# Scores of two pairs of heads in one run of products, in a hybrid encoder trunk

## The chip, the cores and the metric

The kernel runs on one core of a Trainium2 chip. The metric is device time of one execution in microseconds (us). Engines are called PE (TensorE, matrix products), DVE (VectorE), ACT (ScalarE), POOL (GpSimd) and SP (SyncE, which issues the loads).

## The reference

Two layers over a sequence of 256 tokens with 1024 channels, in float32. Each layer projects its input once and gives the parts to three kinds of attention: 6 forgetting heads, 5 stick-breaking heads and 5 sparse heads with an indexer, all 64 wide. Their outputs are gated, merged and projected; a squared-ReLU MLP with a gated embedding follows.

```python
h = x @ w_in[i]
o_fox = fox_attention(fq, fk, fv, log_f)            # softmax(q k + c_q - c_k), causal
o_sb = stick_breaking_attention(sq, sk, sv)         # exp(log_sigmoid(z) + sum of log_sigmoid(-z'))
o_dsa = dsa_attention(dq, dk, dv, iq, ik, iw)       # softmax over the keys that an indexer picks
merged = (gates[:, :, 0] * (o_fox @ w_up_fox[i]) + gates[:, :, 1] * (o_sb @ w_up_sb[i])
          + gates[:, :, 2] * (o_dsa @ w_up_dsa[i]))
x = layer_norm(ALPHA * x + merged @ w_out[i])
ffn = square(relu(x @ w_ff_in[i])) @ w_ff_out[i]
x = layer_norm(ALPHA * x + ffn + sigmoid(x @ w_ple_gate[i]) * (p[i] @ w_ple[i]))
```

## The kernel before

Every product of two float32 matrices is made of three products of rounded halves (`mm3`, line 179): a high and a low part of each operand. ACT makes the high part (a cast, line 164), DVE the low part (a subtraction, line 165); `split` does both. Weights come in units through three rings of five buffers: `wr` (raw), `wh` (high), `wl` (low). So behind each unit on PE stand a load, a cast on ACT and a subtraction on DVE, and the cast waits until PE has given back the `wh` buffer of five units earlier.

PSUM has eight banks. Four are `pg`, the sums of the large projections; four are `ps`, for all small results: scores, transposes, values. `ps()` hands its four banks out in turn, so the fifth tile takes the bank of the first and has to wait until the last reader of that one is done.

The order of the work in a layer is built by generators. `gemm()` yields the units of the large projections in the order of `PRODUCTS`; a loop advances the jobs of the list `JOBS` by one step each for every 550 columns of projection (`PACE`). Jobs are `fox0`, `fox2`, `fox4` (forgetting heads 0 and 1, 2 and 3, 4 and 5), `sb0`, `sb2`, `sb4` (stick-breaking heads, two, two and one), `dsa0`, `dsa1`, `dsa3` (sparse heads 0; 1 and 2; 3 and 4), and others for the decay sums, the indexer and transposes. So small attention steps stand between the products of the weight stream on PE. Each engine then runs its own list in a fixed order.

The steps that matter here:

- The scores of a pair of heads. A head is 64 wide, so one product fills half of the rows of PE's array; `mm3s` (line 186) issues the products of two heads in turn, one on each half, into two `ps` banks. For forgetting and sparse heads this stands at the top of `softmax_heads`; for forgetting heads two further products (line 782) add the decay. For each query tile there are three products a head: first 128 keys wide, then 256. For stick-breaking heads it stands at the top of `sb_heads`.
- The softmax of a head (lines 787 to 794): DVE adds the mask and takes a minimum (787), ACT the exponential (790), DVE the reciprocal and the scaling (792, 794). Then PE transposes (line 199), ACT and DVE split, and `values` multiplies with v.
- Softplus and masks of a stick-breaking head (lines 879 to 886), on ACT, DVE and POOL.
- `values` for stick-breaking head 4 and sparse head 0 leaves its result in two `ps` banks; ACT copies it out (line 761) and DVE takes the rest of the low half (line 762).
- Rotations of the projections (lines 515 to 524) on DVE and POOL; line 573 is PE's product of the turned and split part.

The values of sparse head 0 and of stick-breaking head 4 are made just ahead of the scores of sparse heads 1 and 2; line 573 comes some 15 us after the scores of forgetting heads 2 and 3.

Of the kernel before, what the change touches and what calls it, by code (L numbers as in the profile page):

```python
# [10 lines left out]
F32 = mybir.dt.float32  # L11
# [5 lines left out]
P = 128  # L17
# [5 lines left out]
H_FOX, H_SB, H_DSA, H_IDX = 6, 5, 5, 8  # L23
# [29 lines left out]
def hybrid_trunk(ctx, tc, x, p, w_in, b_forget, w_up_fox, w_up_sb, w_up_dsa, w_out,  # L53
# [10 lines left out]
    def nm(s):  # L64
        uid[0] += 1
        return f"{s}_{uid[0]}"

    def ps():
        return psp.tile([P, 512], F32, tag="ps", name=nm("ps"), bufs=4)
# [24 lines left out]
    def small(w, dt=F32):  # L94
        return act.tile([P, w], dt, tag="small", name=nm("small"), bufs=24)
# [86 lines left out]
    def mm3s(outs, start, stop):  # L182

        for i in range(3):
            for o, a, b in outs:
                nc.tensor.matmul(o, a[i == 2], b[i == 1], start=start and i == 0, stop=stop and i == 2)  # L186
# [9 lines left out]
    def transpose_to(dst, src_list):  # L196

        for i, s in enumerate(src_list):
            tr = nc.tensor.transpose(dst[:, i * P:(i + 1) * P], s, ident)  # L199
            if pinned[0]:  # L200
                tc.keep_in_program_order(tr)
# [280 lines left out]
    mfox = cst.tile([P, 384], F32, name="mfox")  # L482
# [24 lines left out]
    for l in range(L):  # L507
# [158 lines left out]
        M = {}  # L666
# [101 lines left out]
        def t3k(dt=F32R):  # L768
            return act.tile([P, 2, 384], dt, tag="t3k", name=nm("t3k"), bufs=T3K)

        def softmax_heads(n, heads, mask, at_once=False):

            pr = t3k(F32)
            tiles = ((0, slice(0, P)), (1, slice(P, 3 * P)))
            ss = [ps() for _ in heads]
            for t, sl in tiles:
                nk = (t + 1) * P
                mm3s([(s[:, sl], [a[:, t * P:(t + 1) * P] for a in qT], [a[:, 0:nk] for a in kT])
                      for s, (qT, kT, _) in zip(ss, heads)], True, heads[0][2] is None)
                for s, (_, _, extra) in zip(ss, heads):  # L780
                    if extra is not None:
                        nc.tensor.matmul(s[:, sl], extra[0][:, t * P:(t + 1) * P], extra[1][:, 0:nk],
                                         start=False, stop=True)
            for i, s in enumerate(ss):
                mn = small(8)
                for t, sl in tiles:
                    nc.vector.tensor_tensor_reduce(pr[:, i, sl], s[:, sl], mask(t), 1.0, 3e38,
                                                   ALU.add, ALU.min, mn[:, t:t + 1])
                for t, sl in tiles:
                    nc.scalar.activation(pr[:, i, sl], pr[:, i, sl], AF.Exp, bias=mn[:, t:t + 1],  # L790
                                         scale=-1.0, accum_out=mn[:, 2 + t:3 + t])
                nc.vector.reciprocal(mn[:, 4:6], mn[:, 2:4])
                for t, sl in tiles:
                    nc.vector.tensor_scalar(pr[:, i, sl], pr[:, i, sl], mn[:, 4 + t:5 + t], None,
                                            op0=ALU.mult)
                yield
            pT = (t3k(), t3k())
            for i in range(len(heads)):
                q = ps()

                transpose_to(q, [pr[:, i, c * P:(c + 1) * P] for c in range(3)])
                split(q[:, 0:384], pT[0][:, i, :], pT[1][:, i, :])
                last[0] = pT[0].bitcast(F32)[:, i, 0:1]
                if not at_once or i == len(heads) - 1:
                    yield
            values(n, len(heads), pT)
            yield

        def fox_heads(h0):
            def part(i, h):  # L810
                r0 = (h % 2) * 64
                blk = i * 3 + h // 2
                return [a[r0:r0 + 64, (blk % 2) * T:(blk % 2 + 1) * T] for a in fT[blk // 2]]

            def sums(h):
                r = slice((h % 2) * 64, (h % 2) * 64 + 64)
                return sel[r, h // 2, :], cT[r, :]

            return softmax_heads(h0, [(part(0, h), part(1, h), sums(h)) for h in (h0, h0 + 1)],
                                 lambda t: mfox[:, 0:P] if t == 0 else mfox[:, P:3 * P])  # L820

        def dsa_heads(hs):
            def part(h):
                r0 = (h % 2) * 64
                if h < 4:
                    qT = [a[r0:r0 + 64, (h // 2) * T:(h // 2 + 1) * T] for a in dqT]
                else:
                    qT = [a[0:64, :] for a in dq4]
                return qT, [a[r0:r0 + 64, :] for a in dkT], None
            return softmax_heads(H_FOX + H_SB + hs[0], [part(h) for h in hs],  # L830
                                 lambda t: M[t][:, :(t + 1) * P], at_once=hs[-1] == H_DSA - 1)


        def sb_unit(kb):
# [19 lines left out]
        def strict(a, m):  # L854

            for i in range(m):
                v = a[:, i, :].rearrange("p (c t) -> p c t", t=P)[:, 0:3:2, :]
                nc.gpsimd.affine_select(out=v, in_=v, compare_op=ALU.is_gt, fill=0.0, base=0,
                                        pattern=[[0, 2], [1, P]], channel_multiplier=-1)

        def sb_heads(hs):
            m = len(hs)
            u, sp, sph, spl = t3k(F32), t3k(F32), t3k(), t3k()
            zs, qk = [ps() for _ in hs], []
            for h in hs:
                r0 = (h % 2) * 64
# [3 lines left out]
                else:  # L870
# [2 lines left out]
                  for z, (qT, kT) in zip(zs, qk)], True, True)  # L873
            mm3s([(z[:, T:T + P], [a[:, P:T] for a in kT], [a[:, P:T] for a in qT])
                  for z, (qT, kT) in zip(zs, qk)], True, True)
            for i, z in enumerate(zs):
                z = z[:, 0:384]
                e = u[:, i, :]
                nc.scalar.activation(e, z, AF.Abs)
                nc.scalar.activation(e, e, AF.Exp, scale=-1.0)  # L880
                nc.scalar.activation(e, e, AF.Ln, bias=1.0)
                nc.vector.scalar_tensor_tensor(sp[:, i, :], z, 0.0, e, op0=ALU.max, op1=ALU.add)
                nc.vector.scalar_tensor_tensor(e, z, 0.0, e, op0=ALU.min, op1=ALU.subtract)
                strict(sp[:, i:i + 1, :], 1)
                nc.scalar.copy(sph[:, i, :], sp[:, i, :])
                nc.vector.tensor_sub(spl[:, i, :], sp[:, i, :], sph[:, i, :].bitcast(F32))
                yield
# [28 lines left out]
        m = {}  # L916
# [111 lines left out]
        for h in (0, 2, 4):  # L1028
            jobs[f"fox{h}"] = (("fox", "fv"), lambda h=h: fox_heads(h))
        for hs in ((0, 1), (2, 3), (4,)):  # L1030
            jobs[f"sb{hs[0]}"] = (("sb", "sv"), lambda hs=hs: sb_heads(hs))
# [13 lines left out]
        while more or todo or flight:  # L1045
# [13 lines left out]
            while more and cols < PACE:  # L1059
                n = next(units, 0)  # L1060
# [109 lines left out]
        for c in range(NC):  # L1170
            hs = ff_in(c)
# [74 lines left out]
```

## Time and profile before

| | us |
|---|---|
| median of 3 runs | 862.89 (862.77 to 863.03) |
| the profiled execution | 864.14 |
| its span | 862.1 |
| PE busy | 851.7 (99%), 4695 products |
| DVE busy | 641.6 (74%) |
| ACT busy | 471.7 (55%) |
| POOL busy | 67.7 (8%) |

The page's part 1 gives busy time by engine, part 4 the chain of work that ended last, followed back from the last instruction to what released it. The median is what the change is measured by; the profile comes from a single execution, whose own time is in the table. In a timeline a row gives the start, the duration from the first instruction of the row to the end of its last one, the engine, the line, the operation, the tiles and how many instructions the row holds. Products overlap in the pipeline: the distance from one start to the next is what a product costs.

### The profile page before, as it was taken

Reading aid. Unit: us, or ns where it says so; the run is one execution under the profiler, and the core shown is the slowest. Engines: PE = TensorE matmul, PEld = TensorE weight load, DVE = VectorE, ACT = ScalarE, POOL = GpSimd, SP = SyncE. Lnnn points to the kernel's source line nnn. Section 1 sums busy time; section 2 is a strip of 40 time slices with the busy share of each in tenths; the row PEclk is TensorE's granted clock in tenths of the full one; section 3 lists DMA queues with packets and bytes.
Section 4 is the critical chain, followed back from the end, with each engine's and each line's share of the span. In section 5 each row is a group of like instructions: output and inputs, shape, how many; then the busy total and the mean of one; then the engine's idle time right before and its main releaser. Section 6 shows DMA issues by size and latency. Waiting matters only on the chain.

```text
span 862.1 us, 12992 instructions
## 1 busy us (share of the span) xinstructions
PE 851.7 (99%) x4695; PEld 734.7 (85%) x4695; DVE 641.6 (74%) x1151; ACT 471.7 (55%) x754; POOL 67.7 (8%) x136
## 2 busy tenths in 40 slices
PE   9999999999999999999999999999999999999996
PEld 7999988888888888888889998888888888888885
DVE  5679997779867666666876899968898776666666
ACT  4556667686445454444444566677845544444440
POOL 1012011100011000000100211001002100000100
PEclk9999999999999999999999999999999999999998
DMA  7754765545566656666635557556374656666731
GB/s 263 217 140 120 220 192 164 174 141 170 192 213 190 191 193 194 192 194 206 210 117 161 150 149 226 154 181 175 107 240 142 220 195 189 187 190 193 240 126 49
DMA packets 80529, 154.46 MB, mean 179 GB/s; under 512 B 10321, under 2 KB 26321, under 8 KB 80465
## 3 DMA queue, kind: packets, MB, share of 16 engines
q1 hardware_dynamic: 78432, 148.65, 55.2%
q0 software_dynamic: 1600, 4.46, 1.8%
q8 instruction: 37, 0.61, 0.3%
q10 hardware_dynamic: 432, 0.52, 0.2%
q14 instruction: 28, 0.22, 0.1%
HBM read 152.30 MB, written 1.05 MB: 178 GB/s over the span
## 4 chain that ended last, share of the span: by engine, by line
PE 93%; DVE 3%; ACT 1%; issue 1%; POOL 1%; DMA 0%; DVEq 0%; POOLq 0%; SPq 0%
PE pg L179 50%; PE ps L1128 14%; PE ps L1132 7%; PE pg L245 6%; PE pg L573 2%; PE pg L575 2%; PE pg L576 2%; PE ps L186 2%; PE ps L199 2%; PE ps L179 1%; PE pg L383 1%; DVE wl L165 1%; ACT wh L164 0%; DMA wr<-in_w_in_dram 0%; PE pg L960 0%
## 5 line engine op out<-in xcount | busy, mean ns | idle before, releaser
L165 DVE TENSOR_TENSOR wl<-wr,wh 128x1024 fp32r<-128x1024 f32 (+4 forms) x295 | 334.0, 1143 | 164.4 <-ACT wh L164 163.4
L164 ACT CAST wh<-wr 128x1024 fp32r<-128x1024 f32 (+4 forms) x295 | 288.7, 984 | 293.5 <-PE pg L179 113.7
L179 PE MATMUL pg<-wh,t16k 128*128 128x512 f32 (+4 forms) x784 | 228.2, 366 | 0.2
L179 PE MATMUL pg<-wh,t2k 128*128 128x512 f32 x528 | 165.7, 390 | 0.0
L179 PEld LDWEIGHTS pg<-wh,t16k 128*128 128x128 f32 x784 | 142.8, 188 | 21.6 <-ACT t16k L164 1.0
L179 PE MATMUL pg<-wl,t16k 128*128 128x512 f32 (+4 forms) x392 | 141.8, 362 | 0.0
L1128 PE MATMUL ps<-t16k,wh 128*128 128x512 f32 x512 | 127.8, 391 | 0.0
L179 PEld LDWEIGHTS pg<-wh,t2k 128*128 128x128 f32 x528 | 99.2, 188 | 20.4
L1128 PEld LDWEIGHTS ps<-t16k,wh 128*128 128x128 f32 x512 | 93.1, 189 | 17.3
L179 PE MATMUL pg<-wl,t2k 128*128 128x512 f32 x264 | 102.9, 390 | 0.0
L179 PEld LDWEIGHTS pg<-wl,t16k 128*128 128x128 f32 x392 | 73.7, 188 | 8.6 <-DVE wl L165 0.2
L1132 PEld LDWEIGHTS ps<-t16k,wl 128*128 128x128 f32 x512 | 69.8, 190 | 5.0
L1132 PE MATMUL ps<-t16k,wl 128*128 128x256 f32 x512 | 71.4, 282 | 0.0
L179 PEld LDWEIGHTS pg<-wl,t2k 128*128 128x128 f32 x264 | 49.6, 188 | 9.8
L573 PE MATMUL pg<-t16k,wh 128*128 128x256 f32 x176 | 50.5, 287 | 0.4 <-DVE t16k L165 0.4
L576 PE MATMUL pg<-t16k,wl 128*128 128x256 f32 x176 | 49.8, 283 | 0.0
L575 PE MATMUL pg<-t16k,wh 128*128 128x256 f32 x176 | 49.7, 283 | 0.0
L245 PE MATMUL pg<-wh,t16k 128*128 128x512 f32 x136 | 45.4, 396 | 0.0
L179 PE MATMUL pg<-wh,t1k 128*128 128x512 f32 x112 | 37.3, 397 | 0.0
L573 PEld LDWEIGHTS pg<-t16k,wh 128*128 128x128 f32 x176 | 33.7, 191 | 0.9 <-issue 0.8
L575 PEld LDWEIGHTS pg<-t16k,wh 128*128 128x128 f32 x176 | 33.7, 191 | 0.0
L576 PEld LDWEIGHTS pg<-t16k,wl 128*128 128x128 f32 x176 | 33.7, 191 | 0.0
(210 smaller groups left out, 982.2 us busy)
## 6 DMA issues: line engine op xcount, KB each, us to landing
wr<-in_w_ff_in_dram SPq DMA_DIRECT2D x64, 512.0 KB, 4.2
wr<-in_w_ff_out_dram SPq DMA_DIRECT2D x64, 512.0 KB, 3.8
wr<-in_w_in_dram SPq DMA_DIRECT2D x46, 512.0 KB, 4.4
wr<-in_w_in_dram SPq DMA_DIRECT2D x32, 384.0 KB, 3.8
wr<-in_w_out_dram SPq DMA_DIRECT2D x16, 512.0 KB, 4.1
wr<-in_w_ple_gate_dram SPq DMA_DIRECT2D x16, 512.0 KB, 4.3
wr<-in_w_in_dram SPq DMA_DIRECT2D x16, 256.0 KB, 3.1
wr<-in_w_in_dram SPq DMA_DIRECT2D x8, 390.0 KB, 4.6
```

The costliest lines, as they stand in the source:

```text
L164: a = nc.scalar.copy(hi, src)
L165: b = nc.vector.tensor_sub(lo, src, hi.bitcast(F32))
L179: nc.tensor.matmul(o, l, r, start=start and i == 0, stop=stop and i == 2, skip_group_check=skip)
L186: nc.tensor.matmul(o, a[i == 2], b[i == 1], start=start and i == 0, stop=stop and i == 2)
L199: tr = nc.tensor.transpose(dst[:, i * P:(i + 1) * P], s, ident)
L245: nc.tensor.matmul(*args, **kw)
L383: pin(nc.tensor.matmul(o[t], tok(aT, kb, t)[a], w[b][:, 0, :], start=t not in first.setdefault(id(o), []), stop=stop and i == len(kinds) - ...
L573: nc.tensor.matmul(oi, hi, rh, start=kb == 0 and i % 2 == 0, stop=False, skip_group_check=True)
L575: nc.tensor.matmul(oi, hi, rl, start=False, stop=False, skip_group_check=True)
L576: nc.tensor.matmul(oi, lo, rh, start=False, stop=kb == KB - 1, skip_group_check=True)
L1128: nc.tensor.matmul(pz[i], wt[0][:, kk, i * P:(i + 1) * P], x1_both[:, 2 * u + kk, :], start=u + kk == 0, stop=False, skip_group_check=True)
L1132: nc.tensor.matmul(pz[i][:, 0:T], wt[1][:, kk, i * P:(i + 1) * P], x1T[0][:, 2 * u + kk, :], start=False, stop=2 * u + kk == KB - 1, skip_ ...
```

## The change

The products of the scores become functions of their own (`scores`, `sb_scores`), and the job of one pair issues the scores of the next pair as well: `fox0` those of heads 2 and 3, `sb0` those of heads 2 and 3, `dsa1` those of heads 3 and 4. They are kept in a dictionary until the later job takes them. Four `ps` banks are filled in one run. The products are the same, 4695 of them; from the softmax or softplus on, the later pairs remain in their own jobs.

```diff
--- before.py
+++ after.py
@@ -768,10 +768,10 @@
         def t3k(dt=F32R):
             return act.tile([P, 2, 384], dt, tag="t3k", name=nm("t3k"), bufs=T3K)
 
-        def softmax_heads(n, heads, mask, at_once=False):
-
-            pr = t3k(F32)
-            tiles = ((0, slice(0, P)), (1, slice(P, 3 * P)))
+        tiles = ((0, slice(0, P)), (1, slice(P, 3 * P)))
+
+        def scores(heads):
+
             ss = [ps() for _ in heads]
             for t, sl in tiles:
                 nk = (t + 1) * P
@@ -781,7 +781,13 @@
                     if extra is not None:
                         nc.tensor.matmul(s[:, sl], extra[0][:, t * P:(t + 1) * P], extra[1][:, 0:nk],
                                          start=False, stop=True)
-            for i, s in enumerate(ss):
+            return ss
+
+        def softmax_heads(n, heads, mask, at_once=False, ss=None):
+
+
+            pr = t3k(F32)
+            for i, s in enumerate(ss or scores(heads)):
                 mn = small(8)
                 for t, sl in tiles:
                     nc.vector.tensor_tensor_reduce(pr[:, i, sl], s[:, sl], mask(t), 1.0, 3e38,
@@ -806,6 +812,8 @@
             values(n, len(heads), pT)
             yield
 
+        fox_ss, sb_zs, dsa_ss = {}, {}, {}
+
         def fox_heads(h0):
             def part(i, h):
                 r0 = (h % 2) * 64
@@ -816,8 +824,15 @@
                 r = slice((h % 2) * 64, (h % 2) * 64 + 64)
                 return sel[r, h // 2, :], cT[r, :]
 
-            return softmax_heads(h0, [(part(0, h), part(1, h), sums(h)) for h in (h0, h0 + 1)],
-                                 lambda t: mfox[:, 0:P] if t == 0 else mfox[:, P:3 * P])
+            def heads(h0):
+                return [(part(0, h), part(1, h), sums(h)) for h in (h0, h0 + 1)]
+
+
+            if h0 == 0:
+                fox_ss[0] = scores(heads(0))
+                fox_ss[2] = scores(heads(2))
+            return softmax_heads(h0, heads(h0), lambda t: mfox[:, 0:P] if t == 0 else mfox[:, P:3 * P],
+                                 ss=fox_ss.pop(h0, None))
 
         def dsa_heads(hs):
             def part(h):
@@ -827,8 +842,12 @@
                 else:
                     qT = [a[0:64, :] for a in dq4]
                 return qT, [a[r0:r0 + 64, :] for a in dkT], None
+            if hs[0] == 1:
+                dsa_ss[1] = scores([part(h) for h in hs])
+                dsa_ss[3] = scores([part(h) for h in (3, 4)])
             return softmax_heads(H_FOX + H_SB + hs[0], [part(h) for h in hs],
-                                 lambda t: M[t][:, :(t + 1) * P], at_once=hs[-1] == H_DSA - 1)
+                                 lambda t: M[t][:, :(t + 1) * P], at_once=hs[-1] == H_DSA - 1,
+                                 ss=dsa_ss.pop(hs[0], None))
 
 
         def sb_unit(kb):
@@ -858,9 +877,8 @@
                 nc.gpsimd.affine_select(out=v, in_=v, compare_op=ALU.is_gt, fill=0.0, base=0,
                                         pattern=[[0, 2], [1, P]], channel_multiplier=-1)
 
-        def sb_heads(hs):
-            m = len(hs)
-            u, sp, sph, spl = t3k(F32), t3k(F32), t3k(), t3k()
+        def sb_scores(hs):
+
             zs, qk = [ps() for _ in hs], []
             for h in hs:
                 r0 = (h % 2) * 64
@@ -873,6 +891,17 @@
                   for z, (qT, kT) in zip(zs, qk)], True, True)
             mm3s([(z[:, T:T + P], [a[:, P:T] for a in kT], [a[:, P:T] for a in qT])
                   for z, (qT, kT) in zip(zs, qk)], True, True)
+            return zs
+
+        def sb_heads(hs):
+            m = len(hs)
+            if hs[0] in (0, 4):
+                sb_zs[hs[0]] = sb_scores(hs)
+            if hs[0] == 0:
+
+                sb_zs[2] = sb_scores((2, 3))
+            zs = sb_zs.pop(hs[0])
+            u, sp, sph, spl = t3k(F32), t3k(F32), t3k(), t3k()
             for i, z in enumerate(zs):
                 z = z[:, 0:384]
                 e = u[:, i, :]
```

On PE at the forgetting heads the run of heads 0 and 1 ended so, with the projection (`pg_700`) behind it:

```order
L186 MATMUL ps_739<-t2k_688,t2k_683 128x256
L186 MATMUL ps_740<-t2k_688,t2k_683 128x256
L782 MATMUL ps_739<-cT,sel 128x256
L782 MATMUL ps_740<-cT,sel 128x256
L179 MATMUL pg_700<-wh_767,t16k_147 128x320
L179 MATMUL pg_700<-wl_768,t16k_147 128x320
L179 MATMUL pg_700<-wh_767,t16k_147 128x320 x2
```

and it is followed by the other pair now (`ps_756`, `ps_757`):

```order
L186 MATMUL ps_738<-t2k_688,t2k_683 128x256
L186 MATMUL ps_739<-t2k_688,t2k_683 128x256
L782 MATMUL ps_738<-cT,sel 128x256
L782 MATMUL ps_739<-cT,sel 128x256
L186 MATMUL ps_756<-t2k_694,t2k_682 128x128 [waits Activation_49]
L186 MATMUL ps_757<-t2k_694,t2k_682 128x128 [waits PE_49]
L186 MATMUL ps_756<-t2k_695,t2k_682 128x128 [waits DVE_49]
```

The 16 products of the second pair stood 52 rows further on, behind three transposes at line 199, and have moved ahead of five units of the projection. In the new place it waits for ACT's and DVE's parts of its operands.

On PE at the sparse heads, the end of the run of heads 1 and 2 and what came next, before:

```order
L186 MATMUL ps_2145<-t1k_353,t2k_356 128x256
L186 MATMUL ps_2146<-t1k_353,t2k_356 128x256
L179 MATMUL pg_2106<-wh_2169,t16k_147 128x512
L179 MATMUL pg_2106<-wl_2170,t16k_147 128x512
L179 MATMUL pg_2106<-wh_2169,t16k_147 128x512 x2
```

and now, with `ps_2158` and `ps_2159` for heads 3 and 4:

```order
L186 MATMUL ps_2144<-t1k_353,t2k_356 128x256
L186 MATMUL ps_2145<-t1k_353,t2k_356 128x256
L186 MATMUL ps_2158<-t1k_353,t2k_355 128x128 [waits DVE_49]
L186 MATMUL ps_2159<-t1k_353,t1k_357 128x128 [waits DVE_49]
L186 MATMUL ps_2158<-t1k_354,t2k_355 128x128
L186 MATMUL ps_2159<-t1k_354,t1k_357 128x128
L186 MATMUL ps_2158<-t1k_353,t2k_356 128x128
```

The second pair stood at rows that come 26 later, behind two units of the projection and the values of two stick-breaking heads. The `ps` tiles before the run are `ps_2126` (values of sparse head 0) and `ps_2135` (values of stick-breaking head 4); `ps_2158` and `ps_2159` are the fifth and the sixth tile from there and take their banks, so both first products have a wait for DVE.

On DVE at the same place, in the new kernel:

```order
L165 TENSOR_TENSOR t3k_2061<-ps_2062,t3k_2060 128x384 [waits Activation_49]
L936 TENSOR_TENSOR t3k_2081<-t3k_1984,t3k_2080 128x384 [waits DVE_49,Activation_49]
L165 TENSOR_TENSOR wl_2287<-wr_2283,wh_2286 128x1024 [waits DMAHW1_49,DMAHW2_49,PE_49,Activation_49]
L165 TENSOR_TENSOR wl_2328<-wr_2324,wh_2327 128x1024 [waits DMAHW4_49,DMAHW3_49,Activation_49]
L762 TENSOR_TENSOR t1k_370<-ps_2126,t1k_370 64x256 [waits Activation_49]
L762 TENSOR_TENSOR t1k_369<-ps_2135,t1k_369 64x256 [waits Activation_49]
L793 ISA t3k_2172,small_2173<-ps_2144,mt_1410 128x128 [waits DVE_49,PE_49]
```

The two reads of those banks (line 762) stand behind two weight splits, as they did before; line 793 is line 787 of before.

## Rows read from the trace of the kernel before

**Rows 1.** The chain that ended last, by engine (the page's part 4)

```profile
PE 93%; DVE 3%; ACT 1%; issue 1%; POOL 1%; DMA 0%; DVEq 0%; POOLq 0%; SPq 0%
```

**Rows 2.** PE's waits in the whole span: who waited for whom, us, times, longest

```profile
PE pg L573 <- DVE t16k L165: 0.4, 2, 0.2
```

**Rows 3.** Timeline of PE, stick-breaking heads 2 and 3: start, duration, instructions, idle before

```profile
135.57 0.39 PE L179 MATMUL pg<-wh,t16k 128*128 128x512 f32 x1
135.89 0.90 PE L186 MATMUL ps<-t2k,t2k 64*128 64x256 f32 x12
136.72 0.50 PE L179 MATMUL pg<-wh,t16k 128*128 128x512 f32 x1
137.06 0.40 PE L179 MATMUL pg<-wl,t16k 128*128 128x512 f32 x1
```

**Rows 4.** Timeline of PE, the weight stream behind that run

```profile
139.37 0.62 PE L179 MATMUL pg<-wh,t16k 128*128 128x512 f32 x2
139.82 0.39 PE L179 MATMUL pg<-wl,t16k 128*128 128x512 f32 x1
```

**Rows 5.** Timeline of PE, forgetting heads 2 and 3

```profile
63.79 0.55 PE L186 MATMUL ps<-t2k,t2k 64*128 64x128 f32 x6
...
64.90 0.39 PE L179 MATMUL pg<-wh,t16k 128*128 128x264 f32 x1
```

**Rows 6.** Timeline of PE, sparse heads 3 and 4

```profile
173.76 0.32 PE L186 MATMUL ps<-t1k,t2k 64*128 64x128 f32 x1
...
174.32 0.28 PE L186 MATMUL ps<-t1k,t2k 64*128 64x256 f32 x1
...
174.43 0.28 PE L186 MATMUL ps<-t1k,t2k 64*128 64x256 f32 x1
...
174.65 0.50 PE L179 MATMUL pg<-wh,t16k 128*128 128x512 f32 x1
```

**Rows 7.** Timeline of PE, sparse heads 1 and 2

```profile
166.18 0.95 PE L186 MATMUL ps<-t1k,t2k 64*128 64x128 f32 x12
167.06 0.50 PE L179 MATMUL pg<-wh,t16k 128*128 128x512 f32 x1
```

**Rows 8.** Timeline of DVE beside the run of sparse heads 1 and 2

```profile
165.80 2.36 DVE L165 TENSOR_TENSOR wl<-wr,wh 128x1024 fp32r<-128x1024 f32 x2 [0.39 <-ACT wh L164]
168.19 0.77 DVE L762 TENSOR_TENSOR t1k<-ps,t1k 64x256 fp32r<-64x256 f32 x2
```

**Rows 9.** Timeline of ACT at the same place

```profile
166.62 0.64 ACT L761 CAST t1k<-ps 128x256 fp32r<-128x256 f32 x2
```

**Rows 10.** Timeline of PE, the second layer's run of sparse heads 1 and 2

```profile
589.23 0.95 PE L186 MATMUL ps<-t1k,t2k 64*128 64x128 f32 x12
```

**Rows 11.** Timeline of DVE beside it

```profile
591.24 0.77 DVE L762 TENSOR_TENSOR t1k<-ps,t1k 64x256 fp32r<-64x256 f32 x2
```

**Rows 12.** Timeline of DVE ahead of the forgetting heads: the last split of their operands

```profile
53.93 0.42 DVE L165 TENSOR_TENSOR t2k<-pg,t2k 128x256 fp32r<-128x256 f32 x1
```

**Rows 13.** Timeline of PE, forgetting heads 0 and 1

```profile
54.24 0.55 PE L186 MATMUL ps<-t2k,t2k 64*128 64x128 f32 x6
```

**Rows 14.** Timeline of ACT, the last of the weight casts up to 64 us

```profile
63.61 0.83 ACT L164 CAST wh<-wr 128x768 fp32r<-128x768 f32 x1 [0.62 <-PE pg L179]
```

**Rows 15.** Timeline of DVE from there to PE's wait

```profile
61.78 4.25 DVE L165 TENSOR_TENSOR wl<-wr,wh 128x768 fp32r<-128x768 f32 x4
...
69.81 0.36 DVE L515 TENSOR_TENSOR t<-pg,rope 128x192 f32<-128x192 f32 x1 [0.31 <-POOL t2k L522]
```

**Rows 16.** Timeline of PE at its wait

```profile
79.73 0.36 PE L573 MATMUL pg<-t16k,wh 128*128 128x256 f32 x1 [0.19 <-DVE t16k L165]
```

**Rows 17.** Timeline of ACT, index scores and stick-breaking heads 0 and 1

```profile
113.71 1.11 ACT L686 ACTIVATE t2k<-ps 128x512 f32<-128x512 f32 x2
...
131.06 0.51 ACT L885 CAST t3k<-t3k 128x384 fp32r<-128x384 f32 x1 [0.61 <-POOL t3k L858]
```

**Rows 18.** A stretch behind PE's last product: us, busy by engine, granted clock, DMA share, GB/s

```profile
854.10:856.60 2.50, 0.00 (x0) 0.00 (x0) 2.38 (x6) 0.00 (x0) 0.55 (x1) 1.00 0.00 0
```

## Prediction

> **What bounds the kernel now.** I read the chain that ended last first: TensorE (PE) holds 93% of the span [rows 1], so a microsecond saved on PE is saved in full, and one in which PE waits is lost in full, unless another engine ends last at that place. Next came PE's waits over the whole program: its largest repeated one is at line 573, behind a VectorE (DVE) split, 0.4 us in two times, once a layer [rows 2]. The forgetting heads must pass that place. Then I read PE around the score runs, and last DVE and ScalarE (ACT) beside them. Measured against no change, about 0.2% can be told (1.73 us): under 861.16 us is faster, over 864.62 us slower.
>
> **What a run of scores costs.** Products of 512 columns follow each other by about 0.23 us: the two at 139.37 and the next at 139.82 in [rows 4] are 0.45 apart. In [rows 3], around the stick-breaking run the last such product starts at 135.57 and the run at 135.89, 0.09 more than that; the run lasts 0.83 to the next full-height product; the one after comes 0.34 later, 0.11 too much. So the run takes 0.09 + 0.83 + 0.11 = 1.03 us from the stream, and 0.20 of it lies outside the run. The run of forgetting heads 2 and 3 lasts 1.11 [rows 5], that of sparse heads 3 and 4 0.89 [rows 6]; with the same 0.20 they take 1.31 and 1.09. Inside a run, products on the two halves follow by 0.11 (174.32 to 174.43 in [rows 6]); with the change, 8 pairs of them join the forgetting run and 6 each of the two others. I take 0.11 to 0.12 for a pair: 0.92, 0.69 and 0.69 us added at the earlier place. Without a wait the change saves 1.31 - 0.92 = 0.39, 1.03 - 0.69 = 0.34 and 1.09 - 0.69 = 0.40 us: 1.13 a layer, 2.26 in both.
>
> **Sparse heads: a wait that is not there now.** Before, two runs of two heads stand 7.6 us apart (166.18 in [rows 7], 173.76 in [rows 6]). Now the second follows the first, and needs two more banks of the four that `ps` hands out in turn. Those are the banks of the two tiles before the run: the values of sparse head 0 and of stick-breaking head 4. They come free when DVE's two subtractions at line 762 have read them, and the order of DVE puts these behind two weight splits of 128x1024. The splits run from 165.80, the subtractions from 168.19, 0.77 us for two, so the second ends at 168.96 [rows 8]. ACT's copies out of the same banks start at 166.62 and take 0.64 for two [rows 9]: they are not the late ones. PE is done much earlier. Its run starts at 166.18 [rows 7]; six pairs (the first slower by some 0.05 than 0.11 to 0.12) bring it to about 166.98 for the next pair. With nothing for the hand-over the second run begins at 168.96: **1.98 us of stall**. It then lasts as the first does, 0.88 to the next full-height product [rows 7], so that product starts at 169.84 where it now starts at 167.06: +2.78. Less the 1.09 that leaves at 173.76, the layer becomes **1.69 us longer**, and not 0.40 shorter.
>
> Does anything shift this? ACT and DVE reach the splits from work that PE's products set going shortly before, so what PE saves earlier moves them along, and the order of DVE from that work to line 762 is the same in both kernels. DVE can be earlier than in its rows by its 0.39 us of idle ahead of the first split [rows 8] at most. The second layer has the same distances: the run at 589.23 [rows 10], the subtractions at 591.24 [rows 11], 2.01 apart, as 166.18 and 168.19 are. Behind the waiting product the whole weight stream is queued on PE; DVE goes on, since the scores of heads 1 and 2 are there, and it only loses the first scores of 3 and 4 until PE writes them. The 1.09 of the later run cannot be had back elsewhere, as PE has no idle there.
>
> **A rule beside it.** The row shows that DVE still holds a bank 2 us after PE wants it [rows 8]. The Trainium skill, TensorEngine Tiling (Array Packing), Gotcha 1: PSUM Pressure, says that row tiles write to different banks and so raise the pressure on them. The rule makes no difference between the three runs. By it alone none of them would gain, and the sum would be 2 x 1.69 = 3.4 us, 866.3 us. What follows takes it for the sparse run alone.
>
> **Forgetting heads.** The second pair's operands are split by 54.35 (53.93 + 0.42 [rows 12]), before the merged run needs them at about 55.2 (its first half starts at 54.24 [rows 13] and lasts 0.92). No wait, so PE saves 0.39 once the later run has gone. But between the two places PE is 0.92 late, and ACT's weight casts follow PE: the one at 63.61 waited 0.62 for PE [rows 14]. It would end at 65.36 and not 64.44, so that the last of the four DVE splits ends at about 66.38 and not 66.03 (61.78 + 4.25 [rows 15]): DVE starts the rotations and softmax up to PE's wait at 79.73 [rows 16] 0.35 late. In them it has idle time, 0.31 of it in one wait for GpSimd at 69.81 [rows 15]. I take that as the cover: 0.35 - 0.31 = +0.04 at the place where PE waits for DVE anyway, so the 0.39 is lost there. Bounds: -0.39 (DVE keeps up wholly) and +0.35 (no cover). +0.04 lies where DVE bounds, and the wait of [rows 16] says that it does.
>
> **Stick-breaking heads.** The second pair's banks last held index scores and the turned operands of the sparse heads; they were read by about 114.8 (113.71 + 1.11 [rows 17]), 9 us before the run. No wait: -0.34. But the softplus of heads 2 and 3 comes earlier on ACT, and a weight cast that stood ahead of the first pair's two copies is put behind them and behind the first steps of the second pair; the later copy waited for GpSimd until 131.06 [rows 17], so the cast ends at about 133. PE takes the low part of that weight at 139.82 [rows 4]; DVE's split needs 1 to 2 us in between, so some 4 us of cover remain, and without it PE would wait there. Bounds 0 and -0.34; I take -0.34, since both covers are several us long.
>
> **The sum.** Per layer 0.04 - 0.34 + 1.69 = +1.39; twice, **+2.8 us**. The profiled execution took 864.14 us, 1.25 over the median of the three runs, so the sum is 866.9 on its scale and 862.89 + 2.8 = **865.7 us** on the median's. With the upper bound of the forgetting term (0.31 more a layer) it is 866.3, with its lower bound and a stall shorter by 0.39 it is 864.0.
>
> **Rivals.**
>
> *The forgetting gain passes.* DVE catches up between 66 and 79 us, as PE does, and the wait at line 573 keeps its length. Then -0.39 in place of +0.04: +0.96 a layer, 864.8 us. For it speaks that DVE has waits there at all; against it that PE has waited for DVE there in both layers [rows 2].
>
> *The stall is shorter.* DVE reaches line 762 0.39 earlier in each layer and the forgetting gain passes too: 864.8 - 0.8 = 864.0 us, too near to the time before to be told from it. Against it: the casts on ACT that DVE follows do not move against PE.
>
> *The banks are free in time, and it is faster.* The scores need the banks only after ACT has read them, or line 762 comes ahead of the splits. If ACT's copies were the last readers (167.26 [rows 9]), the stall would be 0.3 us and the sum 862.89 - 2.26 + 0.6 = 861.2 us, or 860.6 with no stall at all. It decides where the stall in a layer is under 1.13 us (0.70 with the forgetting gain lost). Against it: the new order gives both first products of the second pair a wait for DVE, and line 762 stands behind the splits there.
>
> *The clock falls in the pause.* In 2.5 us without a product behind PE's last one the granted clock stayed 1.00, which is 2.4 GHz [rows 18]. The pause here is 1.98. If it fell to the other level, 1.2 GHz, every microsecond there would cost 0.5: 2 us of it a layer would give 865.7 + 2.0 = 867.7 us. The Trainium skill, TensorE: Matmul & The Clock Gate, What's actually happening, has PE fall to its lower clock after an idle stretch; no row here shows it for so short a one.
>
> **How the numbers follow.** The forecast has 0.57, as each of its waits stands in an order that is fixed before the run. The forgetting gain passing has 0.15, the falling clock (or another wait of that size that I do not see) 0.07; all three are slower: 0.79 together. The shorter stall has 0.10, mostly within 0.2%. The free banks have 0.11, faster. The range 864.0 to 867.2 holds the forecast, its bounds and the first two rivals, and leaves out the last two, 0.18.
>
> **What would show it.** On PE, the second sparse pair should stand about 2 us after the first, with DVE line 762 (the same number there) named as the releaser, in both layers, and the runs at 64, 136 and 174 us gone. PE's wait at line 573 should stay about as long as it is. If the second sparse pair follows at once, the forecast is wrong and the time is near 861; if PE's wait at line 573 disappears, the forgetting term is wrong.

## The result, and the profile after

The changed kernel took 869.25 us (median of 6 runs, 867.62 to 870.86) against 862.96 us (6 runs) of the kernel before on the same chip: **1.007 times as long, 95% interval 1.0057 to 1.0083, 6.3 us more**. The direction was as forecast; the size was not: 865.7 was forecast, and 869.25 lies above the range of 864.0 to 867.2. The profiled execution took 869.22 us.

Parts 1 and 4 of the page of the changed kernel: busy time, share of the span and instructions by engine, and the chain that ended last.

```profile
PE 852.3 (98%) x4695; PEld 736.2 (85%) x4695; DVE 642.1 (74%) x1151; ACT 472.7 (54%) x754; POOL 67.6 (8%) x136
...
PE 92%; DVE 3%; ACT 2%; issue 1%; DMA 1%; POOL 0%; DVEq 0%; POOLq 0%
```

PE's busy time grew by 0.6 us only (from 851.7), so the page alone does not tell where 6 us went. PE's waits do, in part (us in total, times, longest); the counterpart of before is [rows 2].

```profile
PE ps L186 <- DVE t1k L762: 3.1, 2, 1.5
PE pg L573 <- DVE t16k L165: 2.1, 2, 1.1
```

The first row is the forecast stall, with the releaser that was forecast, once in each layer. The second is the wait of [rows 2], grown from 0.4 to 2.1. But 3.1 + 1.7 = 4.8 of lost time, less three savings in each layer, is not 6.3: something more was lost while PE was busy. So I measured three stages on PE, each from the start of a product in front of the change's place to the start of the same product behind it, in both layers (us, layer 1 and layer 2):

| stage | from | to | before | after | forecast a layer | measured |
|---|---|---|---|---|---|---|
| forgetting | last 320-column product ahead of heads 0 and 1 | product of line 573 [rows 16] | 25.73, 25.71 | 26.20, 26.19 | +0.04 | +0.47, +0.48 |
| stick-breaking | last 512-column product ahead of heads 0 and 1 | the low product of 139.82 [rows 4] | 16.21, 16.21 | 15.84, 15.84 | -0.34 | -0.37, -0.37 |
| sparse | second of the two sets of values ahead of heads 1 and 2, 165.18 before | third product of the up projection, behind the old run of heads 3 and 4, 178.29 before | 13.11, 13.07 | 16.42, 16.44 | +1.69 | +3.31, +3.37 |

The sum is +6.9 us, within the interval of the ratio (4.9 to 7.2 us). The spans themselves, 862.1 and 867.5, differ by less, because the profiled execution of the changed kernel reached the first of these places 1.36 us earlier.

**Stick-breaking** went as forecast. The timeline of PE in the changed kernel shows one run of 24 products in place of two of 12, with no wait around it [rows 3]:

```profile
122.70 0.39 PE L179 MATMUL pg<-wh,t16k 128*128 128x512 f32 x1
123.02 1.59 PE L186 MATMUL ps<-t2k,t2k 64*128 64x256 f32 x24
124.54 0.50 PE L179 MATMUL pg<-wh,t16k 128*128 128x512 f32 x1
```

**Sparse heads.** The timelines of PE and of DVE in the changed kernel at the merged run; the counterparts are [rows 7, 8].

```profile
164.91 0.95 PE L186 MATMUL ps<-t1k,t2k 64*128 64x128 f32 x12
167.40 0.32 PE L186 MATMUL ps<-t1k,t2k 64*128 64x128 f32 x1 [1.54 <-DVE t1k L762]
167.74 0.32 PE L186 MATMUL ps<-t1k,t1k 64*128 64x128 f32 x1
...
168.43 0.41 PE L186 MATMUL ps<-t1k,t1k 64*128 64x256 f32 x1
...
168.99 0.79 PE L179 MATMUL pg<-wh,t16k 128*128 128x512 f32 x1
169.58 0.63 PE L179 MATMUL pg<-wl,t16k 128*128 128x512 f32 x1
170.00 1.05 PE L179 MATMUL pg<-wh,t16k 128*128 128x512 f32 x2
```

```profile
164.53 2.36 DVE L165 TENSOR_TENSOR wl<-wr,wh 128x1024 fp32r<-128x1024 f32 x2 [0.39 <-ACT wh L164]
166.92 0.77 DVE L762 TENSOR_TENSOR t1k<-ps,t1k 64x256 fp32r<-64x256 f32 x2
```

Line 762 starts 2.01 us after the run does, as it did before (168.19 - 166.18 in [rows 7, 8]). The first product of the second pair goes as soon as the first subtraction has given back its bank, after 1.54 us of wait; the next, which needs the second bank, is released 0.34 later. And then something that stood nowhere in the forecast's sum: the products that follow are slow. The second 512-column product starts 0.59 behind the first, where it is 0.34 behind a run at the usual speed (136.72 to 137.06 in [rows 3]), and the third 0.42 behind the second, where 0.23 is usual. The columns of the next view (stretch, us, busy by engine PE, PEld, DVE, ACT, POOL, granted clock, DMA share, GB/s) show why.

```profile
165.90:167.40 1.50, 0.00 (x0) 0.00 (x1) 1.47 (x3) 0.08 (x1) 0.00 (x0) 1.00 0.85 290
167.40:168.10 0.70, 0.68 (x7) 0.54 (x9) 0.67 (x4) 0.00 (x0) 0.00 (x0) 1.00 0.85 234
168.10:171.50 3.40, 3.40 (x15) 2.69 (x14) 3.15 (x20) 3.18 (x13) 0.00 (x0) 0.50 0.86 236
171.60:176.00 4.40, 4.40 (x21) 3.60 (x21) 2.48 (x8) 1.81 (x6) 0.00 (x0) 1.00 0.18 68
```

```profile
594.80:597.90 3.10, 3.10 (x11) 2.32 (x8) 2.85 (x18) 2.88 (x13) 0.00 (x0) 0.50 0.86 253
597.90:598.10 0.20, 0.20 (x2) 0.17 (x1) 0.20 (x3) 0.20 (x2) 0.00 (x0) 0.50 0.99 358
```

PE is without a product for 1.50 us, works again for 0.70 us at a granted clock of 1.00 (2.4 GHz), and then gets 0.50 (1.2 GHz) for 3.4 us, in which it is busy all the time. Layer 2 shows the same for at least the 3.3 us of its two rows. That is time which counts as busy on the page and as a wait in no view. It may not have come in both layers of each execution: the fastest of the six runs, 867.62 us, is 1.6 us under the median and had a mean clock of 0.996, where the others had 0.993 or 0.994 and the profiled execution of before 0.997.

### The profile page after: what moved, and what is told of

Read it like the earlier page. It is cut to its first block, busy times and chain, and to the rows that moved or that the text cites. A ratio compares the mean times of both kernels' runs of the same rounds, so it can differ in the third digit from the quotient of the medians.

```text
span 867.5 us, 12990 instructions
## 1 busy us (share of the span) xinstructions
PE 852.3 (98%) x4695; PEld 736.2 (85%) x4695; DVE 642.1 (74%) x1151; ACT 472.7 (54%) x754; POOL 67.6 (8%) x136
## 4 chain that ended last, share of the span: by engine, by line
PE 92%; DVE 3%; ACT 2%; issue 1%; DMA 1%; POOL 0%; DVEq 0%; POOLq 0%
PE pg L179 51%; PE ps L1157 14%; PE ps L1161 7%; PE pg L245 6%; PE pg L573 2%; PE pg L575 2%; PE pg L576 2%; PE ps L186 2%; PE ps L199 2%; PE ps L179 1%; PE pg L383 1%; DMA wr<-in_w_up_dsa_dram 1%; ACT wh L164 1%; DVE wl L165 1%; DVE t1k L165 0%
```

## The experiments

Each was timed beside the kernel before on its own chip; stage times are those of the table above.

### Each part of the change alone

Three kernels keep one part each. The blocks that two of them lose (`sb_alone` loses both of these, `dsa_alone` the first; `fox_alone` the second):

```diff
-            if h0 == 0:
-                fox_ss[0] = scores(heads(0))
-                fox_ss[2] = scores(heads(2))
...
-            if hs[0] == 1:
-                dsa_ss[1] = scores([part(h) for h in hs])
-                dsa_ss[3] = scores([part(h) for h in (3, 4)])
```

and for `fox_alone` and `dsa_alone` the stick-breaking scores go back:

```diff
-            if hs[0] in (0, 4):
-                sb_zs[hs[0]] = sb_scores(hs)
-            if hs[0] == 0:
-
-                sb_zs[2] = sb_scores((2, 3))
+            sb_zs[hs[0]] = sb_scores(hs)
```

> Only the stick-breaking scores of heads 2 and 3 join the run of heads 0 and 1; forgetting and sparse heads as before. Theory (banks free, one entry and exit of a run saved per layer): 0.7 us less than before, about 862.2, no new wait on PE. Rival (the earlier softplus on ACT puts weight casts late and PE waits for them between 124 and 157 us): no gain or a loss, 862.9 or more, with a PE wait behind a cast there.

> Only the forgetting scores of heads 2 and 3 join the run of heads 0 and 1. Theory now (ACT's and DVE's lists for these heads come out in another order, and PE's wait at line 573 grows by 0.8 us a layer, more than the 0.4 saved): 0.9 us more than before, about 863.8, with PE's waits at line 573 some 1.7 us longer in sum. Rival 1, the forecast's cover: 863.0. Rival 2, the loss seen in the changed kernel comes only together with the other two parts: 862.1.

> Only the sparse scores of heads 3 and 4 join the run of heads 1 and 2. Theory (PE waits 2 us for the banks behind line 762, and the granted clock falls behind that pause): about 6.4 us more than before, 869.3, of it 1.7 a layer from the wait less the run saved and 1.4 a layer from products at half clock. Rival (the clock's fall belongs to the three parts together, or to chance): 1.7 us a layer, 866.3, with a granted clock of 1.00 behind the pause.

| kernel | us | before | ratio (95%) | its stage |
|---|---|---|---|---|
| sb_alone | 863.15 | 863.92 | 0.999 (0.9981 to 0.9999) | 15.84 |
| fox_alone | 864.82 | 863.92 | 1.0009 (1.0 to 1.0017) | 26.18, 26.18 |
| dsa_alone | 869.83 | 863.92 | 1.0073 (1.0057 to 1.0088) | 16.38, 16.43 |

Each part alone moves its own stage by what it does in the whole change, and the other stages by 0.03 at most. So the parts add up, the forgetting loss is its own, and nearly all of the 6.3 us is the sparse part.

### The pause filled with other products

To part the wait from the clock, `dsa_filled` puts 16 products that nobody reads between the two sparse pairs, into unused columns of the first pair's banks; `dsa_half_filled` puts 8 there. Their operand `lfh` is zero at the start of the program; by this place 48 of its 128 columns hold logarithms of forget gates, so the expectations are wrong to call them products of zeros.

```diff
                 dsa_ss[1] = scores([part(h) for h in hs])
+                for i in range(16):
+                    s = dsa_ss[1][i % 2]
+                    tc.keep_in_program_order(nc.tensor.matmul(
+                        s[:, 384:512], lfh[:, 0, :], lfh[:, 0, :], start=True, stop=True))
                 dsa_ss[3] = scores([part(h) for h in (3, 4)])
```

> As the kernel with the sparse scores alone, and between its two pairs 16 more products of 128 columns of zeros into columns of the first pair's banks that nothing reads, so that PE has work in most of the pause; the wait for line 762 ends at the same time. Theory (the slow products behind the pause are PE's lower clock, brought on by PE standing still): granted clock 1.00 throughout, about 866.4. Rival (the products behind the pause are slow for another reason, as loads or bank traffic that meet there): slow as before them, about 869.3.

> As the sparse scores alone with products of zeros between its pairs, but 8 and not 16: PE stands still for about 0.9 us and not 2. The wait for line 762 ends at the same time. Theory (the clock falls after a pause as long as 2 us and not after every pause): granted clock 1.00 and about the time of the 16, 3.6 over before. Rival (any pause at this place brings the clock down): 0.50 for some us behind it, about 6 over before.

`dsa_filled` took 867.63 us against 863.92, ratio 1.004 (1.0026 to 1.0054). Its four runs lie between 866.6 and 867.75, those of `dsa_alone` between 869.5 and 870.98. PE in its timeline, and the stretches behind:

```profile
165.99 2.00 PE L846 MATMUL ps<-lfh 128*128 128x128 f32 x16
167.92 0.32 PE L186 MATMUL ps<-t1k,t2k 64*128 64x128 f32 x1
...
168.82 0.50 PE L179 MATMUL pg<-wh,t16k 128*128 128x512 f32 x1
```

```profile
167.90:168.80 0.90, 0.90 (x13) 0.77 (x12) 0.88 (x7) 0.49 (x3) 0.00 (x0) 1.00 1.37 218
168.80:172.20 3.40, 3.40 (x17) 2.81 (x16) 3.15 (x19) 3.19 (x14) 0.00 (x0) 1.00 0.87 263
```

The second pair starts 2.82 us after the first (165.10). In the changed kernel the product that needs the second bank stood 2.83 behind the first pair (167.74 - 164.91), so the banks still set the time, but the clock stays at 1.00. The loads are as busy as in the slow stretch of the changed kernel (DMA share 0.87 and 0.86), so they are not what makes the products slow. The stage takes 14.84 and 14.88: +1.73 and +1.81, against the forecast's +1.69. The wait was priced right; **the clock is the rest, 16.4 - 14.86 = 1.5 us a layer**. The medians of the totals give less, 869.83 - 867.63 = 2.2 us for both layers, from four runs each that spread by more than 1 us.

`dsa_half_filled` leaves a wait of 0.50 in each layer (and the next product, on the second bank, starts 0.34 behind the one that waited). It took 867.88 us against 864.28, ratio 1.0047 (1.0031 to 1.0062). In its profile the stage took 14.88 in layer 1 and 16.44 in layer 2, and the clock tells the two apart:

```profile
169.90:173.00 3.10, 3.10 (x18) 2.45 (x15) 2.85 (x18) 2.89 (x13) 0.00 (x0) 1.00 0.89 280
594.70:597.90 3.20, 3.20 (x12) 2.49 (x12) 2.95 (x20) 2.99 (x14) 0.00 (x0) 0.50 0.82 226
```

So 0.5 us without a product, in the same place of the same program, was followed by the lower clock in one layer and not in the other; its five runs spread from 867.03 to 870.6, with mean clocks from 0.998 to 0.993. What decides between the two stays open.

### What holds the forgetting heads

Two suspects: ACT, whose weight casts now stand ahead of the exponentials of heads 2 and 3, or DVE, whose list is full. `fox_ordered` puts two of those casts (with their DVE splits) behind the exponentials again; `fox_exp` holds the exponentials.

```diff
+            with ExitStack() as st:
+                if kb in (0, 2):
+                    st.enter_context(tc.issue_after(fox_exp[kb // 2].ins))
-            split(raw, hi, lo)
+                split(raw, hi, lo)
```

> As the forgetting heads alone, but two weight casts on ACT are queued behind the exponentials of heads 2 and 3, so that ACT's list has the order of before there. Theory (of the growth of PE's wait at line 573, 0.2 to 0.35 us a layer come from casts that the new order put ahead of the exponentials): 0.4 to 0.7 us less than the forgetting heads alone, 0.2 to 0.5 over before; wait at line 573 down from 2.1 to about 1.5 us. Rival (the whole growth comes from PE reaching the casts 0.9 us later): as the forgetting heads alone, 0.9 over before, wait 2.1.

It took 864.75 us against 864.28, ratio 1.0007 (0.9998 to 1.0016), and the stage 26.14 and 26.13, 0.05 less than `fox_alone`; the wait at line 573 is 2.0 in sum. That is what its rival said, so the order on ACT falls as the cause. `fox_less_dve` takes work from DVE instead: one weight unit a layer has no low part of its own and uses another unit's, which saves one 128x640 subtraction.

```diff
+            if kb == 1:
+                nc.scalar.copy(hi, raw)
+                return hi, sb_lo[0]
```

`before_less_dve` is the kernel before with the same edit.

> As the forgetting heads alone, but of the stick-breaking weights one unit in a layer has no low part of its own on DVE (its products use the low part of another unit): one DVE subtraction of 128x640, 0.74 us from start to start, is left out ahead of PE's wait at line 573. Theory (DVE's list, busy all the way, sets the end of that wait): wait down from 2.1 to about 0.6 us in sum, 1.5 us less than the forgetting heads alone, 0.6 under before. Rival (ACT or POOL set it, and DVE only stands last in the list): wait 1.5 us or more.

> The kernel before with the same subtraction left out. Theory (DVE sets the wait here too, by little): the wait of 0.4 us goes, 0.5 to 0.7 us under before. So the forgetting heads merged, with that subtraction out in both, are equal to this or some 0.1 us better, where they are 0.9 worse with it. Rival: no change, the wait stays.

PE at line 573, in the timelines of the changed kernel, of `fox_ordered` and of `fox_less_dve`, each in a fence of its own:

```profile
78.85 0.36 PE L573 MATMUL pg<-t16k,wh 128*128 128x256 f32 x1 [1.06 <-DVE t16k L165]
```

```profile
80.09 0.35 PE L573 MATMUL pg<-t16k,wh 128*128 128x256 f32 x1 [1.00 <-DVE t16k L165]
```

```profile
79.57 0.36 PE L573 MATMUL pg<-t16k,wh 128*128 128x256 f32 x1 [0.20 <-DVE t16k L165]
```

With one subtraction less (0.82 us) the stage takes 25.32, 0.40 under before: the whole forecast saving of 0.39. So DVE's list sets the end of this stage, and the saving on PE is there but hidden behind it. In the kernel before the same edit saves only 0.05 in each layer. DVE's list does not bound the stage alone there: with the subtraction out, DVE waits for ACT's cast of a later unit, and PE's wait shrinks only from 0.19 and 0.18 to 0.14 and 0.12. DVE in `before_less_dve`:

```profile
73.55 0.82 DVE L165 TENSOR_TENSOR wl<-wr,wh 128x640 fp32r<-128x640 f32 x1 [0.44 <-ACT wh L164]
```

The total was less clear than the stage: `fox_less_dve` took 863.68 against 863.93, ratio 0.9996 (0.9987 to 1.0005), `before_less_dve` 864.72, ratio 1.0008 (0.9999 to 1.0017); both profiles show a new wait of 0.4 us of PE for DVE at line 179 in layer 2. I had not foreseen that wait, and the expected gain of `before_less_dve` did not come.

`sb_fox_pool` (the changed kernel without the sparse part) gives that subtraction to GpSimd.

```diff
+            if kb == 1:
+                nc.scalar.copy(hi, raw)
+                nc.gpsimd.tensor_sub(lo, raw, hi.bitcast(F32))
+                return hi, lo
```

> Stick-breaking and forgetting scores merged, sparse heads as before; the low part of one unit of the stick-breaking weights in a layer is made on GpSimd and not on DVE, ahead of PE's wait at line 573. Theory (DVE's list sets that wait, and one subtraction less in it gives the forgetting heads their 0.4 us a layer back): forgetting heads -0.4, stick-breaking heads -0.37 in each layer, 1.5 us under before. Rival (GpSimd's subtraction is slower than 3 us or slows DVE beside it, so that PE waits for it at line 576 or at line 573 as long as without it): -0.7 at best, or a loss.

864.14 us against 863.94, ratio 1.0 (0.9991 to 1.0008); the wait at line 573 grew to 1.2, and the forgetting stage took 26.27 and 26.31. The timelines of POOL and of DVE show what happened:

```profile
71.44 1.58 POOL L860 TENSOR_TENSOR wl<-wr,wh 128x640 fp32r<-128x640 f32 x1
```

```profile
71.73 1.97 DVE L165 TENSOR_TENSOR wl<-wr,wh 128x640 fp32r<-128x640 f32 x1
...
73.70 0.80 DVE L165 TENSOR_TENSOR wl<-wr,wh 128x640 fp32r<-128x640 f32 x1
```

DVE's own subtraction of the same size takes 1.97 beside GpSimd's and 0.80 without it; the one beside it ends at 73.70, 0.68 after GpSimd's (71.44 + 1.58 = 73.02). What GpSimd took over, DVE lost again.

### The banks read first

`sb_dsa_evicted` keeps the stick-breaking and sparse parts and puts the two weight splits behind the reads of the two banks; `freed` holds the copy and the subtraction of the later of the two.

```diff
-            split(raw, *wt)
+            with tc.issue_after(freed[0].ins), tc.issue_after(freed[1].ins):
+                split(raw, *wt)
```

> Stick-breaking and sparse scores merged, forgetting heads as before; the splits of the weights of the first two units of the up projection are queued on ACT and DVE behind the copies and subtractions at lines 761 and 762. Theory (those two reads stand behind the splits and nothing else holds the banks): no wait of the second sparse pair over 0.1 us, granted clock 1.00, 0.34 + 0.40 us saved in a layer: 1.5 us under before. Rival (the banks or the operands are late for another reason, or the splits are late for PE now): a wait of the second pair or of the up projection of 0.5 us or more, no gain.

862.9 us against 864.28, ratio **0.9983 (0.9974 to 0.9992): faster than the kernel before, and the lowest ratio of all that ran**. Its DVE and PE timelines:

```profile
165.39 0.43 DVE L762 TENSOR_TENSOR t1k<-ps,t1k 64x256 fp32r<-64x256 f32 x1 [0.38 <-ACT t1k L761]
166.29 0.43 DVE L762 TENSOR_TENSOR t1k<-ps,t1k 64x256 fp32r<-64x256 f32 x1 [0.47 <-ACT t1k L761]
```

```profile
165.78 1.02 PE L186 MATMUL ps<-t1k,t2k 64*128 64x128 f32 x13
166.77 0.32 PE L186 MATMUL ps<-t1k,t1k 64*128 64x128 f32 x1
...
167.65 0.50 PE L179 MATMUL pg<-wh,t16k 128*128 128x512 f32 x1
```

The long wait is gone and the clock fall with it. But the stage took 13.04 in both layers, 0.07 and 0.03 under before and not 0.40: the second read ends at 166.29 + 0.43 = 166.72, and the second bank's first product goes at 166.77, some 0.2 later than PE alone would have it (165.78 and the 0.80 of the prediction for six pairs). Where the rest of the missing 0.35 goes was not tried. The stages save 0.74 + 0.10 = 0.84 us, nearly all of it in the stick-breaking part. That the total came out 1.4 under, close to the 1.5 of the theory, is luck: the sparse gain that the theory counted is not there, and the interval overlaps that of `sb_alone`.

`all_ordered` joins `sb_dsa_evicted` with `fox_ordered`; `all_pool_evicted` is the changed kernel with the edits of `sb_dsa_evicted` and `sb_fox_pool`.

> The whole change, with both reorderings: casts behind the exponentials of forgetting heads 2 and 3, splits behind lines 761 and 762. Theory: 1.5 us saved by the other two parts as without the forgetting heads, and 0.2 to 0.5 lost by these: 1.0 to 1.3 under before. Rival (the three parts act on each other): more than 0.5 us away from the sum of the parts.

> The whole change with two repairs: the same subtraction on GpSimd, and the splits of the up projection's first weights behind lines 761 and 762. Theory: the sum of the parts, -0.4 forgetting, -0.37 stick-breaking, -0.06 sparse in a layer: 1.7 us under before. Rival (the sparse part costs more when the layer runs ahead, or its pause brings the clock down in some executions): less than 1.0 under before.

864.05 us against 864.28, ratio 0.9997 (0.9989 to 1.0006), and 864.13 against 863.94, ratio 1.0003 (0.9994 to 1.0012). Neither gain of the theories came. The stages of the two profiled executions add up to -0.1 and +0.3 us. With the stall mended, the three merged runs together are no change: the forgetting part gives back what the stick-breaking part saves.

## Why the prediction was right and wrong

**The stall: right.** Its place, its releaser (line 762 behind two weight splits) and both layers came as forecast. The row of the wait says 1.54 where the forecast said 1.98, since the first product needs only the first of the two banks; the second waits on, and the price of the stage without the clock, +1.73 and +1.81, is the forecast's +1.69 within 0.12.

**The clock: the step that failed.** The forecast had this as a rival with a chance of 0.07 and set [rows 18] against it: 2.5 us behind the last product at a clock of 1.00. That row was misread. It shows that the fall comes late, not that PE may stand still. The stretches right behind it, in the kernel before and in the changed kernel (whose last product starts at 859.11), were to be had:

```profile
856.80:858.00 1.20, 0.00 (x0) 0.00 (x0) 1.20 (x3) 0.00 (x0) 0.23 (x1) 0.50 0.00 0
```

```profile
862.20:863.40 1.20, 0.00 (x0) 0.00 (x0) 1.20 (x3) 0.00 (x0) 0.25 (x1) 1.00 0.00 0
```

In one the clock has fallen by 856.8, in the other it has not by 863.4, after the same end of the program. A clock that follows its cause late, and not always by the same time, cannot be judged by the pause itself: here it fell 0.7 and 1.0 us after PE had started again. The price failed as well: the rival counted half of the pause's own 2 us, 1.0 a layer. The slow stretch is a separate one, 3.4 us long in layer 1 and at least 3.3 in layer 2, and costs 1.5 a layer. That is 3.1 us in both, most of the 3.5 us by which the forecast missed. The Trainium skill, TensorE: Matmul & The Clock Gate, What's actually happening, has PE fall to its lower clock after an idle stretch; the runs agree in the direction, and in every profiled layer of the changed kernel and of `dsa_alone` the lower clock followed a pause of 1.5 us.

**Forgetting heads: the mechanism right, the size wrong.** With the change, DVE bounds the place where PE waits, as the term said, and the whole saving goes into that wait. But the forecast took this from the wait of [rows 16] in the kernel before, and that row did not show it: there one subtraction less on DVE saved 0.05 and not up to 0.19 (`before_less_dve`). The term of +0.04 measured +0.47, above its upper bound of +0.35. DVE's rows of the changed kernel, and behind them the answering rows of before that were not shown, tell the steps:

```profile
65.12 0.54 DVE L165 TENSOR_TENSOR t3k<-ps,t3k 128x384 fp32r<-128x384 f32 x1
...
68.57 0.36 DVE L515 TENSOR_TENSOR t<-pg,rope 128x192 f32<-128x192 f32 x1 [0.31 <-POOL t2k L522]
...
69.17 0.55 DVE L165 TENSOR_TENSOR t3k<-ps,t3k 128x384 fp32r<-128x384 f32 x1
...
70.19 0.82 DVE L165 TENSOR_TENSOR wl<-wr,wh 128x640 fp32r<-128x640 f32 x1
71.13 0.17 DVE L798 RECIPROCAL small<-small 128x2 f32<-128x2 f32 x1
```

```profile
65.95 0.54 DVE L165 TENSOR_TENSOR t3k<-ps,t3k 128x384 fp32r<-128x384 f32 x1
...
67.75 0.17 DVE L792 RECIPROCAL small<-small 128x2 f32<-128x2 f32 x1 [0.38 <-ACT t3k L790]
...
70.96 0.55 DVE L165 TENSOR_TENSOR t3k<-ps,t3k 128x384 fp32r<-128x384 f32 x1
71.43 0.82 DVE L165 TENSOR_TENSOR wl<-wr,wh 128x640 fp32r<-128x640 f32 x1
72.16 0.16 DVE L792 RECIPROCAL small<-small 128x2 f32<-128x2 f32 x1
```

Counted from PE's anchor (54.01 before, 52.65 now, so 1.36 apart), DVE is 65.12 + 1.36 - 65.95 = 0.53 late behind the four splits, not 0.35. By 68.57 it is 0.12 late (69.81 in [rows 15]), so most was absorbed, but not by the wait for GpSimd that the forecast named: that is 0.31 still. What went is the wait of 0.38 for ACT at 67.75. Up to the split that releases PE another 0.36 is lost. DVE's list is in another order there: the split of 69.17 stood between the minimum and the weight split before (70.96) and stands ahead of the minimum now. So the reciprocal follows its own minimum too soon and goes 0.94 after the weight split of 70.19, where 0.73 lay between them before. The rest of the 0.36 is spread over smaller gaps; this reading of rows was not tried by a run of its own. What the runs show is that DVE sets the wait (`fox_less_dve`) and that the order of ACT's casts does not (`fox_ordered`). The bound failed because it moved DVE's list as a whole, while the change reorders it.

**Stick-breaking heads: right.** -0.37 for -0.34, with no wait; both covers held. The added products cost what the forecast took for a pair.

**The other rivals.** Banks free in time: not so in the changed kernel; even where they are read first (`sb_dsa_evicted`), a stage gains 0.05 and not 0.40. Forgetting gain passes: only with DVE relieved. Of the 4.1 us between the stages' sum of 6.9 and the forecast's 2.8, the clock has 3.1, the forgetting term 0.9 and the rest 0.1.

## What to carry to other kernels

When a run is made longer so that it takes more buffers of a ring at once, read who gives back each of those buffers, and what stands ahead of that read on its engine: here two weight splits of 1.2 us each on DVE decided the result, and reading the banks first took the sparse stage from 3.3 us lost to 0.05 gained. Price a pause of PE at its length and, as a term of its own, at the slow stretch that may follow when PE already works again; look for that in the granted clock behind a pause, since no view of waits shows it. A saving on PE counts only up to the next place where PE waits for another engine, so find out first whether that engine's list can follow.

## What the runs showed of the hardware

- The granted clock fell from 1.00 to 0.50 0.7 and 1.0 us after PE had resumed, and stayed there for 3.4 us and at least 3.3 us of unbroken work. It followed a pause of 1.5 us in both layers, one of 0.5 us in one layer of two.
- Sixteen products into unused columns kept the clock at 1.00 through the same wait and gained 1.5 us a layer in the stage: products that compute nothing can be worth their time.
- A DVE subtraction with both inputs in SBUF took 1.97 us beside a GpSimd subtraction and 0.80 without. The Trainium skill, SBUF — State Buffer, SBUF: two separate sides, says that such a DVE operation and a GpSimd operation that reads SBUF share a pair of ports which one of them holds for its whole instruction; the rows agree, as DVE's ended 0.68 us after GpSimd's.
- Executions of nearly the same program reached the same early product up to 1.7 us apart (54.01 before, 52.65 in the changed kernel, 54.36 in `sb_alone`), so stages are compared from anchors, not from the start of the span.
